# Four edits to the order of work in a two-layer decoder kernel: earlier weight sums, an earlier fifth product, both second-branch gates first, small loads on another queue

## The chip, the cores and the metric

The kernel runs on one core of a Trainium2 chip. The metric is device time in microseconds (us) of one execution, median of several. A core has five engines that run their own instruction streams in order and meet only at semaphores: TensorE (PE, matrix products; PEld is its weight load), VectorE (DVE), ScalarE (ACT), GpSimd (POOL) and SyncE (SP, which here only issues DMAs). An engine's stream is fixed when the kernel is built: an instruction that has to wait holds up all that stand behind it on the same engine.

## The reference, cut to what matters

Two layers; x is 256 positions by 2048 channels, all in float32. Each layer:

```
h = RMSNorm(x);  proj = h @ w_in                  # 2048 x 7680: q | k | v | u, v of the gating unit | gates A | gates B
branch_a = window_attention(q, k, v) @ w_attn_branch        # 1024 x 2048
branch_b = (gelu(u) * spatial(gelu(v))) @ w_sgu_branch      # 1024 x 2048
merged = sigmoid(gates A) * branch_a + sigmoid(gates B) * branch_b
x = x + merged @ w_out                                      # 2048 x 2048
h2 = RMSNorm(x);  x = x + (silu(h2 @ w_gate) * (h2 @ w_up)) @ w_down    # 2048 x 5632, twice; 5632 x 2048
```

## The kernel before, in words

**Three products for one.** Each float32 matrix is split into a high part (rounded to the reduced format fp32r) and a low part (what rounding left), and a product is made of three: high with high, high with low, low with high. That is `three`, lines 345 to 348: the lines PE spends its time in. The weights are split as they arrive: ACT rounds a block of 128 x 1024 (`high`, line 226, tile `whi`), DVE subtracts (`low`, line 234, tile `wlo`). The activations lie in `Unit`s, transposed, with tiles `uh`/`ul` for the parts of the whole and `sh`/`sl` for the parts of sums.

**Jobs, parts and steps.** All weights are cut into jobs (lines 101 to 159), each as a rule 1024 output columns wide, run one after the other by `run` (line 350). A job goes through the input rows in units of 512. One unit of a whole kind is four steps of one weight block ("part") each, with 12 matmuls a step. For jobs with m = 1 the first unit is multiplied in Strassen's manner: seven products of six matmuls each in place of four steps of twelve, in the order of `PRODUCTS` (line 89): 11, t1, t2, 21, t3, 22, t4. Three of the weight blocks are taken as they are (11, 21, 22), four are sums that DVE makes in place (`add`, line 218): t1 = 12 - 11 into an own tile, t2 = 22 - t1 over block 11, t3 = 22 - 12 over block 12, t4 = 21 - t2 over t1's tile. Each layer has 21 such jobs: two of the second branch's gates, two of w_out, and all 17 of the feed-forward part. The others (q, k, v, u, first gates, both branch products) are of the whole kind.

Five PSUM banks serve a Strassen unit (lines 357 to 363): `a`, `q`, `x`, `e`, `y`. ACT copies `a` into `x` after 11, into `e` after t2 and into `y` after t3 (line 380), and `q` into a tile `p5` after 21 (line 383), which DVE adds to `e` and `a` (line 386), before c = 1 of the next unit accumulates into them.

**The stream of weights.** `Stream.fill` (line 238) is called ahead of each step with `upto`, the step's number plus 5. It emits highs for parts up to `upto`, lows for parts below `upto`, and sums for parts below `upto + 2`. There are six `whi` and five `wlo` buffers and four raw weight buffers of 1 MB, so the low of a part can run when PE has finished the part five before it. Lows, sums and all else on DVE share its one queue in the order of emission. `load` (line 174) issues the next weight load on SP when the raw buffer's last part has its low emitted.

**Slots.** What follows from a job's result is written out by hand on a count of slots (`tick`, line 296): a whole step counts 1, a Strassen step 0.5. `soon` runs a function behind the next step's fill, `after(n, f)` n slots later. `evicting` (line 277) places the reads of a job's PSUM banks: both row blocks at the next step for the first 512 columns (c = 0), the second row block later for c = 1, and `then` after it (one, two or three slots). A Strassen job that comes next moves these places (`T1_LATE`, `THEN_LATE`).

**From a branch to w_out.** `branch(gb, j, ...)` (line 1010) multiplies a gate by the branch's product (line 1018, two per c), and its `then_` adds the two branches (`merge`, line 1024) and calls `transposed` (line 479): two DVE transposes (line 432), 16 small DMAs on POOL's queue (line 438) into a tile `tt`, and by slot count a split of what landed: ACT's high (line 535) and DVE's low (line 538). For the first 512 columns (`mT[0]`) w_out's Strassen unit needs sums too: `combine` (line 450), in three slots: `first` with four DVE adds (line 462) and ACT's high (line 464), `second` with DVE's low of the whole (line 457, `ul`) and ACT's high of the sums (line 469), `third` with DVE's low of the sums (line 457, `sl`). It starts 6.7 slots behind `then_`.

The order of jobs is written twice and has to agree: the weights in lines 138 to 159, the runs in lines 970 to 1075. Around the change a layer runs: gates A (two jobs), branch A (two), gate B columns 0 to 1023, branch B of these, gate B columns 1024 to 2047, branch B of these, w_out (two), feed-forward.

**The start.** SP issues eight loads of x between the first four weight loads (lines 306 to 312). POOL issues eight small loads (lines 333 and 630 to 634: two norm rows, the sinks, cosine, sine, three blocks of vector rows), which `tables` (slot 7) and `columns` (slot 12) read. `DMA` issues on SP run in order and each waits for the one eight before it (its semaphore) to land.

Of the kernel before, what the change touches and what calls it, by code (L numbers as in the profile page):

```python
# [14 lines left out]
P = 128  # L15
# [16 lines left out]
CW2 = 2 * CW  # L32
# [18 lines left out]
def hybrid_trunk(ctx: ExitStack, tc: tile.TileContext, x, mix_norm, w_in, q_norm, k_norm, sinks,  # L51
                 sgu_ln_g, sgu_ln_b, w_spatial, b_spatial, w_attn_branch, w_sgu_branch, w_out,
                 ffn_norm, w_gate, w_up, w_down, cosine, sine, out):
    nc = tc.nc
# [32 lines left out]
    O_KV, O_U, O_V, O_GATE = QW, QW + 2 * KVW, QW + 2 * KVW + SW, QW + 2 * KVW + 2 * SW  # L87
    NF = FF // CW
    PRODUCTS = ("11", "t1", "t2", "21", "t3", "22", "t4")

    class Job:

# [10 lines left out]
    def load_of(job, u, h=None):  # L103
        ks = slice(u * CW, (u + 1) * CW) if h is None else slice(u * CW + h * 2 * P, u * CW + (h + 1) * 2 * P)
        loads.append((job, [c[ks, :].rearrange("(k p) n -> p k n", p=P) for c in job.cols]))
        return len(loads) - 1

    def add_job(cols, units=None, m=0):
        job = Job(cols, units, m)
        jobs.append(job)  # L110
        held = {}
        for u in job.units[:m]:
            held[u] = load_of(job, u, 0), load_of(job, u, 1)
        for i, name in enumerate(PRODUCTS if m else ()):
            for n, u in enumerate(job.units[:m]):
                a, b = held[u]
                v = {"11": (a, 0), "12": (a, 1), "21": (b, 0), "22": (b, 1), "new": (f"sum{len(jobs)}_{u}", 0)}
                dst, one, two = {"11": ("11", 0, 0), "22": ("22", 0, 0), "21": ("21", 0, 0),
                                 "t1": ("new", "12", "11"), "t2": ("11", "22", "new"),
                                 "t3": ("12", "22", "12"), "t4": ("new", "21", "11")}[name]  # L120
                parts.append((v[dst], one and (v[one], v[two]), b))
                job.steps.append((name, u, n == m - 1))
        for u in job.units[m:]:
            if not job.pair:
                a = load_of(job, u)
# [12 lines left out]
    for l in range(DEPTH):  # L138
        wl = w_in[l]
        for o in (0, None)[::-1 if l == 0 else 1]:  # L140
            add_job([wl[:, o:o + CW2] if o is not None else wl[:, O_KV:O_KV + CW]])
        for o, m in ((O_V, 0), (O_U, 0), (O_GATE, M_GATE[0]), (O_GATE + CW2, M_GATE[1])):
            add_job([wl[:, o:o + CW2]], m=m)
        for i, o in enumerate((0, CW2)):
            add_job([w_attn_branch[l, :, o:o + CW2]], m=M_ATT[i])
        for i, o in enumerate((0, CW2)):
            add_job([wl[:, O_GATE + D + o:O_GATE + D + o + CW2]], m=M_GATE[2 + i])
            add_job([w_sgu_branch[l, :, o:o + CW2]], m=M_SGU[i])
        for o in (0, CW2):
# [12 lines left out]
    for i, (dst, total, newest) in enumerate(parts):  # L162
        for n in (dst[0], newest, *(w[0] for w in total or ())):
            last_use[n] = i

    class Stream:
# [47 lines left out]
        def add(self):  # L214
            dst, total, _ = parts[self.summed]
            self.summed += 1
            if total:
                nc.vector.tensor_tensor(out=self.raw(dst), in0=self.raw(total[0]), in1=self.raw(total[1]),  # L218
                                        op=ALU.subtract)

        def high(self):
            i = len(self.highs)
            raw = self.raw(parts[i][0])
            hi = whigh.tile([P, 2, CW], F32R, tag="hi", name=nm("whi"))
            for k in self.pieces(i):
                nc.scalar.activation(hi[:, k, :], raw[:, k, :], AF.Copy)  # L226
            self.highs.append(hi)
# [101 lines left out]
    neg_half = const.tile([P, 24], F32, name="neg_half")  # L329
    nc.gpsimd.memset(neg_half, -0.5)  # L330

    def bcast(dst, row):
        nc.gpsimd.dma_start(dst, row.unsqueeze(0).to_broadcast([P, row.shape[0]]))


    def rsqrt(dst, src, n):
# [13 lines left out]
    def run(units, done):  # L350
# [17 lines left out]
        for n, (name, u, at) in enumerate(job.steps):  # L368
# [3 lines left out]
            if name != "whole":  # L372
# [5 lines left out]
                if at:  # L378
                    if name in ("11", "t2", "t3"):
                        nc.scalar.activation({"11": x, "t2": e, "t3": y}[name], a, AF.Copy)  # L380
                    elif name == "21":
                        fifth = temp(name="p5")
                        nc.scalar.activation(fifth, q, AF.Copy)
                    elif name == "t4":
                        for d in (e, a):
                            nc.vector.tensor_tensor(out=d, in0=d, in1=fifth, op=ALU.add)  # L386
                if n < len(job.steps) - 1:
                    tick(0.5)
# [238 lines left out]
        nc.vector.tensor_copy(vcols, pv[:, :NV])  # L627

    def vectors():
        nc.gpsimd.dma_start(cs, cosine.rearrange("(t p) h -> p t h", p=P))  # L630
        nc.gpsimd.dma_start(sn, sine.rearrange("(t p) h -> p t h", p=P))
        nc.gpsimd.dma_start(vrows[:NB, :], mix_norm.rearrange("l (k p) -> (l k) p", p=P))
        nc.gpsimd.dma_start(vrows[NB:2 * NB, :], ffn_norm.rearrange("l (k p) -> (l k) p", p=P))
        nc.gpsimd.dma_start(vrows[2 * NB:, :], b_spatial.rearrange("l g i -> (l g) i"))

    after(3, vectors)
    after(12, columns)

    H2 = HD // 2

    class Layer:
# [7 lines left out]

        def vectors(self):  # L650
            l = self.l
            bcast(self.gn[:, 0, :], q_norm[l])
            bcast(self.gn[:, 1, :], k_norm[l])
            bcast(self.snk, sinks[l])

        def fetch(self, i, eng):

# [312 lines left out]
    for l in range(DEPTH):  # L970
# [142 lines left out]
```

## Time and profile before

| | |
|---|---|
| median of 3 runs | 2488.98 us (2488.92 to 2489.47) |
| the profiled execution | 2486.52 us, span 2484.8 us |
| PE busy | 2464.7 us (99%), 11030 matmuls |
| DVE busy | 1901.5 us (77%) |
| ACT busy | 1359.2 us (55%) |
| POOL busy | 479.5 us (19%) |
| granted TensorE clock | 0.999 |
| read from HBM | 475.27 MB, 192 GB/s over the span |

The span runs from the first to the last instruction; the execution's time is 1.72 us longer, and the median of the runs is another 2.46 us above that. In rows of the timeline the columns are start and duration in us, engine, line, operation, the tile written and the tile read, how many, and in brackets the idle time of the engine before it and what ended it. A matmul's duration there is longer than the distance to the next one, since matmuls overlap; distances of starts tell the pace.

### The profile page before, as it was taken

The page shows a single profiled execution, that of the slowest core. Times are in us where ns is not written, and L with a number is a line of the kernel's source. Part 1 is how long each engine was busy: PE and PEld are TensorE (multiplying, and loading weights), DVE is VectorE, ACT ScalarE, POOL GpSimd, SP SyncE. Part 2 cuts the span into 40 slices and gives each one's busy share as a digit, 9 for nine tenths or more (in the row PEclk, how much of TensorE's full clock was granted, in tenths as well). Part 3 has the DMA queues.
Part 4 walks back from the last instruction along what each step waited for, and adds up shares of the span by engine and source line. Part 5 has one row for each costly group of instructions (what it writes and reads, how often), then busy time and mean ns, then how long its engine had stood idle before and what let it go on. Part 6 is the DMA issues. An engine that isn't in the chain of part 4 may idle for free. (4 is left out here: it accounts for less than half of the span.)

```text
span 2484.8 us, 30610 instructions
## 1 busy us (share of the span) xinstructions
PE 2464.7 (99%) x11030; PEld 2023.1 (81%) x11030; DVE 1901.5 (77%) x2135; ACT 1359.2 (55%) x1660; POOL 479.5 (19%) x911
## 2 busy tenths in 40 slices
PE   9999999999999999999999999999999999999999
PEld 7888887788888888888888888877888888888887
DVE  6796667787877787777878956678878776877686
ACT  5455455576655555455654544555756555645554
POOL 1512202231220022002235122022402200220020
PEclk9999999999999999999999999999999999999999
DMA  8645656666565656566676546565756656565654
GB/s 280 227 157 169 204 196 205 205 200 223 195 233 173 234 187 233 191 219 206 216 231 214 166 160 214 192 201 187 251 189 230 211 197 209 196 221 184 213 192 164
DMA packets 161880, 507.71 MB, mean 204 GB/s; under 512 B 22016, under 2 KB 24672, under 8 KB 161728
## 3 DMA queue, kind: packets, MB, share of 16 engines
q1 hardware_dynamic: 133408, 476.87, 56.7%
q0 software_dynamic: 28000, 28.62, 3.8%
q8 instruction: 86, 1.41, 0.2%
q14 instruction: 66, 0.54, 0.1%
q10 hardware_dynamic: 320, 0.27, 0.0%
HBM read 475.27 MB, written 2.10 MB: 192 GB/s over the span
## 5 line engine op out<-in xcount | busy, mean ns | idle before, releaser
L234 DVE TENSOR_TENSOR wlo<-raw,whi 128x1024 fp32r<-128x1024 f32 (+1 forms) x940 | 1129.5, 1217 | 502.7 <-PE acc L347 415.8
L226 ACT ACTIVATE whi<-raw 128x1024 fp32r<-128x1024 f32 (+1 forms) x940 | 983.3, 1056 | 843.0 <-PE acc L348 773.6
L346 PE MATMUL acc<-whi,uh 128*128 128x512 f32 x3164 | 1243.2, 393 | 7.1 <-DVE acc L386 4.6
L347 PE MATMUL acc<-wlo,uh 128*128 128x512 f32 x3164 | 1232.7, 390 | 3.1 <-DVE wlo L234 3.1
L348 PE MATMUL acc<-whi,ul 128*128 128x512 f32 x3164 | 1232.3, 389 | 0.0
L438 POOL DMA_DIRECT2D tt<-blk x800 | 393.1, 498 | 1721.8 <-DVE blk L432 1042.6
L346 PEld LDWEIGHTS acc<-whi,uh 128*128 128x128 f32 x3164 | 594.2, 188 | 146.2 <-DVE acc L386 13.1
L348 PEld LDWEIGHTS acc<-whi,ul 128*128 128x128 f32 x3164 | 594.4, 188 | 125.0
L347 PEld LDWEIGHTS acc<-wlo,uh 128*128 128x128 f32 x3164 | 594.6, 188 | 124.0 <-DVE wlo L234 3.7
L226 ACT ACTIVATE whi<-sum 128x1024 fp32r<-128x1024 f32 x84 | 89.2, 1062 | 96.6 <-PE acc L348 61.2
L346 PE MATMUL acc<-whi,sh 128*128 128x512 f32 x336 | 132.7, 395 | 5.0 <-ACT acc L380 5.0
L347 PE MATMUL acc<-wlo,sh 128*128 128x512 f32 x336 | 131.0, 390 | 0.0
L348 PE MATMUL acc<-whi,sl 128*128 128x512 f32 x336 | 130.9, 390 | 0.0
L234 DVE TENSOR_TENSOR wlo<-sum,whi 128x1024 fp32r<-128x1024 f32 x84 | 102.5, 1221 | 8.7 <-PE acc L347 8.7
L346 PEld LDWEIGHTS acc<-whi,sh 128*128 128x128 f32 x336 | 63.0, 188 | 23.7 <-ACT acc L380 11.1
L380 ACT ACTIVATE acc<-acc 128x512 f32<-128x512 f32 x126 | 73.7, 585 | 10.0 <-PE acc L348 10.0
L348 PEld LDWEIGHTS acc<-whi,sl 128*128 128x128 f32 x336 | 63.1, 188 | 13.4
L347 PEld LDWEIGHTS acc<-wlo,sh 128*128 128x128 f32 x336 | 63.1, 188 | 12.5
L538 DVE TENSOR_TENSOR ul<-tt,uh 128x1024 fp32r<-128x1024 f32 x38 | 46.4, 1222 | 17.9 <-ACT uh L535 16.1
L535 ACT ACTIVATE uh<-tt 128x1024 fp32r<-128x1024 f32 x38 | 40.3, 1059 | 34.6 <-DMA tt<-blk 32.5
L386 DVE TENSOR_TENSOR acc<-acc,p 128x512 f32<-128x512 f32 x84 | 54.1, 689 | 0.0
L218 DVE TENSOR_TENSOR raw<-raw,sum 128x1024 f32<-128x1024 f32 x42 | 51.4, 1224 | 1.4
(134 smaller groups left out, 1055.0 us busy)
## 6 DMA issues: line engine op xcount, KB each, us to landing
raw<-in_w_in_dram SPq DMA_DIRECT2D x112, 1024.0 KB, 5.1
raw<-in_w_down_dram SPq DMA_DIRECT2D x88, 1024.0 KB, 6.7
raw<-in_w_gate_dram SPq DMA_DIRECT2D x80, 1024.0 KB, 6.0
raw<-in_w_up_dram SPq DMA_DIRECT2D x80, 1024.0 KB, 6.2
raw<-in_w_out_dram SPq DMA_DIRECT2D x32, 1024.0 KB, 6.8
tt<-blk POOLq DMA_DIRECT2D x800, 32.0 KB, 5.1
raw<-in_w_attn_branch_dram SPq DMA_DIRECT2D x16, 1024.0 KB, 6.2
raw<-in_w_sgu_branch_dram SPq DMA_DIRECT2D x16, 1024.0 KB, 5.8
```

Source lines behind the costliest of these rows:

```text
L218: nc.vector.tensor_tensor(out=self.raw(dst), in0=self.raw(total[0]), in1=self.raw(total[1]), op=ALU.subtract)
L226: nc.scalar.activation(hi[:, k, :], raw[:, k, :], AF.Copy)
L234: nc.vector.tensor_tensor(out=lo[:, k, :], in0=raw[:, k, :], in1=hi[:, k, :].bitcast(F32), op=ALU.subtract)
L346: nc.tensor.matmul(ps, a, hi, start=first, stop=False, skip_group_check=True)
L347: nc.tensor.matmul(ps, a, lo, start=False, stop=False, skip_group_check=True)
L348: nc.tensor.matmul(ps, b, hi, start=False, stop=last, skip_group_check=True)
L380: nc.scalar.activation({"11": x, "t2": e, "t3": y}[name], a, AF.Copy)
L386: nc.vector.tensor_tensor(out=d, in0=d, in1=fifth, op=ALU.add)
L438: nc.gpsimd.dma_start(blocks(d)[:, :, i] if whole else d[:, i].rearrange("p k t c -> p (k t) c"), src)
L535: nc.scalar.activation(blocks(unit.hi), tv, AF.Copy)
L538: nc.vector.tensor_tensor(out=blocks(unit.lo), in0=tv, in1=blocks(unit.hi).bitcast(F32), op=ALU.subtract)
```

## The change

It has four parts.

1. Sums: each sum gets a lead of its own (t1 and t2: 1, t3: 3, t4: 4 parts more than `upto`, in place of 1 for all), and a condition: the part whose weight block it overwrites (11 for t2, t1 for t4) must have its low emitted. For t1 and t2 the place stays as it was; t3's sum is emitted two fills earlier, beside t2's, and t4's three fills earlier, right behind t1's low. Parts without a sum pass up to `upto + 4`.
2. Fifth product: DVE adds it to `a` and `e`, in this order, behind the matmuls of 22, and no longer to `e` and `a` behind those of t4.
3. Job order: gate B of columns 0 to 1023, gate B of columns 1024 to 2047, then the two branch B jobs, then w_out. Between the `then_` of the first branch B job and w_out there is now one job of eight whole steps; before, there was a gate job as well.
4. Small loads: the eight of the first layer are issued by SP, at slot 1, behind the first four weight loads; the second layer's three stay on POOL, one slot earlier.

```diff
+    SUM_AHEAD = {"t1": 1, "t2": 1, "t3": 3, "t4": 4}
...
-                parts.append((v[dst], one and (v[one], v[two]), b))
+                over = {"t2": "11", "t4": "t1"}.get(name)
+                at[name, u] = len(parts)
+                parts.append((v[dst], one and (v[one], v[two], at.get((over, u), -1), SUM_AHEAD[name]), b))
...
             add_job([wl[:, O_GATE + D + o:O_GATE + D + o + CW2]], m=M_GATE[2 + i])
+        for i, o in enumerate((0, CW2)):
             add_job([w_sgu_branch[l, :, o:o + CW2]], m=M_SGU[i])
...
+        def due(self, upto):
+            if self.summed == len(parts):
+                return False
+            total = parts[self.summed][1]
+            if not total:
+                return self.summed < upto + 4
+            return self.summed < upto + 1 + total[3] and len(self.parts) > total[2]
...
-                elif self.summed < min(upto + 2, n):
+                elif self.due(upto):
                     self.add()
...
-                    elif name == "t4":
-                        for d in (e, a):
+                    elif name == "22":
+                        for d in (a, e):
                             nc.vector.tensor_tensor(out=d, in0=d, in1=fifth, op=ALU.add)
...
     def vectors():
-        nc.gpsimd.dma_start(cs, cosine.rearrange("(t p) h -> p t h", p=P))
+        nc.sync.dma_start(cs, cosine.rearrange("(t p) h -> p t h", p=P))
...
-    after(3, vectors)
+    after(1, vectors)
...
+            eng = nc.gpsimd if l else nc.sync
+            bcast(eng, self.gn[:, 0, :], q_norm[l])
...
-        after(2, pl.vectors)
+        after(1, pl.vectors)
...
         for j in (0, 2):
             gate(gb, j)
+        for j in (0, 2):
             branch(gb, j, spa.sguT, merge)
```

More of the change, by code (lines that the diff above doesn't have):

```diff
@@ L112, in add_job @@
         for u in job.units[:m]:
-            held[u] = load_of(job, u, 0), load_of(job, u, 1)
+                held[u] = load_of(job, u, 0), load_of(job, u, 1)
+        at = {}
         for i, name in enumerate(PRODUCTS if m else ()):
@@ L162, in hybrid_trunk @@
     for i, (dst, total, newest) in enumerate(parts):
-        for n in (dst[0], newest, *(w[0] for w in total or ())):
+        for n in (dst[0], newest, *(w[0] for w in (total or ())[:2])):
             last_use[n] = i
@@ L330, in hybrid_trunk, with bcast @@
     nc.gpsimd.memset(neg_half, -0.5)
-    def bcast(dst, row):
-        nc.gpsimd.dma_start(dst, row.unsqueeze(0).to_broadcast([P, row.shape[0]]))
+    def bcast(eng, dst, row):
+        eng.dma_start(dst, row.unsqueeze(0).to_broadcast([P, row.shape[0]]))
     def rsqrt(dst, src, n):
@@ L629, in vectors @@
     def vectors():
-        nc.gpsimd.dma_start(cs, cosine.rearrange("(t p) h -> p t h", p=P))
[L631 to L634, printed above, removed]
-    after(3, vectors)
+        nc.sync.dma_start(cs, cosine.rearrange("(t p) h -> p t h", p=P))
+        nc.sync.dma_start(sn, sine.rearrange("(t p) h -> p t h", p=P))
+        nc.sync.dma_start(vrows[:NB, :], mix_norm.rearrange("l (k p) -> (l k) p", p=P))
+        nc.sync.dma_start(vrows[NB:2 * NB, :], ffn_norm.rearrange("l (k p) -> (l k) p", p=P))
+        nc.sync.dma_start(vrows[2 * NB:, :], b_spatial.rearrange("l g i -> (l g) i"))
+    after(1, vectors)
     after(12, columns)
@@ L651, in vectors @@
             l = self.l
-            bcast(self.gn[:, 0, :], q_norm[l])
-            bcast(self.gn[:, 1, :], k_norm[l])
-            bcast(self.snk, sinks[l])
+            eng = nc.gpsimd if l else nc.sync
+            bcast(eng, self.gn[:, 0, :], q_norm[l])
+            bcast(eng, self.gn[:, 1, :], k_norm[l])
+            bcast(eng, self.snk, sinks[l])
         def fetch(self, i, eng):
```

## The prediction

> **What bounds the kernel now.** First the page:
>
> ```profile
> span 2484.8 us, 30610 instructions
> PE 2464.7 (99%) x11030; PEld 2023.1 (81%) x11030; DVE 1901.5 (77%) x2135; ACT 1359.2 (55%) x1660; POOL 479.5 (19%) x911
> ```
>
> PE is the bound, and nothing in the change alters its matmuls; only time in which PE waits can go. Next, who waits for whom, on PE and then on ACT:
>
> ```profile
> PE acc L346 <- ACT acc L380: 5.0, 4, 1.4
> PE acc L346 <- DVE acc L386: 4.6, 4, 1.2
> PE acc L347 <- DVE wlo L234: 3.1, 2, 2.5
> ACT whi L226 <- DVE sum L218: 35.4, 38, 2.4
> ```
>
> Four long waits for a bank copy, four for the fifth product, two in the start; and ACT often waits for a sum. These views miss short waits, since matmuls overlap, so I take the pace from the timeline of PE: the first matmul of step t1 in successive Strassen jobs, from gate B of the first layer on.
>
> ```profile
> 330.22 0.39 PE L346 MATMUL acc<-whi,sh 128*128 128x512 f32 x1
> ...
> 394.16 0.39 PE L346 MATMUL acc<-whi,sh 128*128 128x512 f32 x1
> ...
> 461.23 0.39 PE L346 MATMUL acc<-whi,sh 128*128 128x512 f32 x1
> ...
> 461.68 0.39 PE L348 MATMUL acc<-whi,sl 128*128 128x512 f32 x1
> ...
> 506.53 0.39 PE L346 MATMUL acc<-whi,sh 128*128 128x512 f32 x1
> ...
> 549.19 0.39 PE L346 MATMUL acc<-whi,sh 128*128 128x512 f32 x1
> ...
> 591.89 0.39 PE L346 MATMUL acc<-whi,sh 128*128 128x512 f32 x1
> ...
> 634.09 0.39 PE L346 MATMUL acc<-whi,sh 128*128 128x512 f32 x1
> ...
> 677.01 0.39 PE L346 MATMUL acc<-whi,sh 128*128 128x512 f32 x1
> ```
>
> Matmuls start 0.227 us apart (0.45 over two), so a Strassen step lasts 1.36 us and a whole step 2.72. Gate job plus branch job takes 63.94 us the first time and 67.07 the second: the second gate job loses 3.13. From w_out's first job to its second are 45.30, where 591.89 to 634.09 shows 42.20 for the same work: 3.10 lost. The next two lose 0.46 and 0.50 (42.66, 42.70), and 634.09 to 677.01 loses 0.72 (42.92). The job before it, an "up" job that follows a gate job, loses nothing.
>
> Where the big ones come from, in w_out's first job (PE, ACT, DVE):
>
> ```profile
> 466.64 0.50 PE L346 MATMUL acc<-whi,sh 128*128 128x512 f32 x1 [1.17 <-ACT acc L380]
> 475.12 0.50 PE L346 MATMUL acc<-whi,uh 128*128 128x512 f32 x1 [1.21 <-DVE acc L386]
> ```
>
> ```profile
> 464.10 1.06 ACT L226 ACTIVATE whi<-sum 128x1024 fp32r<-128x1024 f32 x1 [2.09 <-DVE sum L218]
> ```
>
> ```profile
> 449.02 1.23 DVE L234 TENSOR_TENSOR wlo<-raw,whi 128x1024 fp32r<-128x1024 f32 x1 [0.36 <-issue]
> 450.28 1.22 DVE L218 TENSOR_TENSOR raw<-raw,sum 128x1024 f32<-128x1024 f32 x1
> ...
> 454.47 1.23 DVE L234 TENSOR_TENSOR wlo<-raw,whi 128x1024 fp32r<-128x1024 f32 x1 [1.49 <-PE acc L347]
> 455.61 1.22 DVE L218 TENSOR_TENSOR raw<-raw,raw 128x1024 f32<-128x1024 f32 x1
> 456.75 1.28 DVE L1018 SCALAR_TENSOR_TENSOR gate<-gate,acc 128x512 f32<-128x512 f32 x2
> 458.06 1.23 DVE L1024 TENSOR_TENSOR gate<-gate,gate 128x1024 f32<-128x1024 f32 x1
> 459.32 1.31 DVE L432 STREAM_TRANSPOSE blk<-gate 128x512 f32<-128x512 f32 x2
> 460.55 2.32 DVE L234 TENSOR_TENSOR wlo<-raw,whi 128x1024 fp32r<-128x1024 f32 x2
> 462.78 1.22 DVE L218 TENSOR_TENSOR sum<-raw,raw 128x1024 f32<-128x1024 f32 x1
> ...
> 474.37 1.29 DVE L386 TENSOR_TENSOR acc<-acc,p 128x512 f32<-128x512 f32 x2
> ```
>
> DVE is late behind the previous job's results; t4's sum runs at 462.78, ACT waits 2.09 for it, and the copy of `a` into `e` stands behind that on ACT: PE waits. Later the adds of the fifth product (474.37) stand behind merge, transposes and a low.
>
> **Gate B's second job.** It now follows a gate job, whose results only ACT reads; no product, merge or transposes lie on DVE there. That is the up-behind-gate pattern (42.20). Gain 3.13 a layer, **-6.3 us**. If two gate jobs do disturb each other, the nearest row is 42.92: -4.8.
>
> **Sums and fifth product in the other Strassen jobs.** t4's sum leaves the crowded stretch (1.14 us, the distance 454.47 to 455.61) for a whole step with 2.72 us of PE time and 2.4 of DVE work, so ACT's high finds it ready and the copies come on time. The adds now stand ahead of merge or transposes. They wait for ACT's `y` copy and for 22's last matmul; behind them on DVE wait only lows for steps five ahead. By the order of jobs five per layer follow an up job (0.72 each) and about five in all follow as the two after w_out's first do (0.48): 10 x 0.72 + 5 x 0.48 = 9.6. I take **-9.1**; bounds 0 (sums come no earlier in fact) and -9.6.
>
> **w_out's first job.** Here the reorder costs. `mT[0]`'s combine, until now hidden in the second gate job's whole steps, has one branch job of eight steps left. By slots `first` falls behind that job's sixth step, `second` behind the seventh, `third` behind the eighth, the last. Prices:
>
> ```profile
> 412.08 0.42 DVE L462 TENSOR_TENSOR sums<-tt 128x256 f32<-128x256 f32 x1
> ...
> 413.67 1.23 DVE L234 TENSOR_TENSOR wlo<-raw,whi 128x1024 fp32r<-128x1024 f32 x1
> ...
> 417.52 1.22 DVE L457 TENSOR_TENSOR sl<-sums,sh 128x1024 fp32r<-128x1024 f32 x1
> ```
>
> Four adds take 1.59, each low 1.14 to 1.22. On the clock of the quoted rows, with distances from them, DVE would run: low 11 at 449.02, t2's sum 450.28, t3's sum 451.42, t1's low 452.55, t4's sum 453.81, the four adds 454.95, t2's low 456.54, two products 457.68, `ul` 458.99, merge 460.14, transposes 461.40, low 21 462.63, `sl` 463.77, done 464.99. The first matmul that reads `sl` is the third of t1, due at 461.68: PE waits 3.3 us. `ul` is done at 460.2, in time for PE's 460.3. From then on PE is late itself: t3's low, 22, t4 and the adds come out 0.3 us or more ahead of it. With 0.2 for short waits the job loses 3.5 in place of 3.1: **+0.8** for two layers. Bounds: 0.5 lost per job if DVE catches up before t1 (-5.2), 6 if it is 2.5 us later than I count (+5.8).
>
> `first` also needs the gather:
>
> ```profile
> 476.95 1.06 ACT L535 ACTIVATE uh<-tt 128x1024 fp32r<-128x1024 f32 x1 [0.64 <-DMA tt<-blk]
> ```
>
> This one landed 16.3 us after its transposes (459.32 + 1.31). `mT[0]`'s transposes would end near 437.6 (ten whole steps ahead of 459.87, plus a low, two products, merge, transposes), so it lands at 453.9, 1.0 us ahead of the adds. A thin cover: each us of lateness beyond it is a us of PE.
>
> A wait of 3.3 us may also cost clock:
>
> ```profile
> 0.00:8.70 8.70, 5.62 (x26) 4.79 (x26) 2.32 (x7) 3.85 (x8) 6.29 (x18) 1.00 0.74 191
> 8.70:12.10 3.40, 3.08 (x7) 2.49 (x8) 0.96 (x2) 1.62 (x3) 0.00 (x0) 0.50 1.04 366
> 12.10:20.00 7.90, 5.35 (x27) 4.20 (x26) 5.40 (x9) 6.28 (x12) 0.00 (x0) 1.00 1.05 407
> ```
>
> (Stretch, length, PE busy with its count, then the other engines, granted clock, DMA.) The clock fell to 0.50 for 3.4 us after a stretch in which PE was busy 5.62 of 8.70 us, but stayed 1.00 across the start's wait of 2.5 us, with 5.35 of 7.90. A fall costs half of 3.4, 1.7 us. Whether 3.3 us suffice depends on what stands around them; I take one fall in two jobs: **+1.7** (bounds 0 and +3.4). The Trainium skill, "TensorE: Matmul & The Clock Gate", section "HAM oscillation — how this bites in real kernels", has it that the clock halves after PE idles for more than about 3.4 us; by that rule 3.3 us would pass in both, and the sum would be 1.7 lower. The trace does not quite agree: PE idled 3.1 us in all ahead of 8.70, in pieces, and the clock fell.
>
> **Small loads.**
>
> ```profile
> 17.54 17.19 SPq L197 DMA_DIRECT2D raw<-in_w_in_dram  x5
> 28.73 2.01 ACT L226 ACTIVATE whi<-raw 128x1024 fp32r<-128x1024 f32 x2
> raw<-in_w_in_dram SPq DMA_DIRECT2D x112, 1024.0 KB, 5.1
> cs<-in_cosine_dram POOLq DMA_DIRECT2D x1, 32.0 KB, 7.0
> ```
>
> They leave POOL, whose next work is far off, and stand on SP ahead of the fifth weight load (17.54). That one may have to wait until a small one lands: an estimate of 17.54 + 7.0 = 24.5 at the latest, and 5.1 for itself, 29.6. ACT first reads it at 28.73, without a wait; 0.9 us there is covered, since a high stands about five steps ahead of its matmuls. `tables` reads the small ones only at slot 7, seven steps of 2.72 us or more behind the first. So **0**, between +1.0 (cover gone) and -0.5 (the first loads no longer share the DMA engines with the small ones, but PE's 2.5 us in the start are a wait for DVE).
>
> **Sum.** -6.3 - 9.1 + 0.8 + 1.7 + 0 = -12.9 us. The profiled execution (2486.52, span 2484.8) would come to 2473.6; it lies 2.46 below the median, so the median goes from 2488.98 to **2476**.
>
> **Rivals.** *DVE catches up at w_out* (its engine has idle time in the whole steps before; against it, five lows, four sums and the rest of the list above, 18 us of work in 13.6): w_out loses 0.5, no clock falls, -6.3 - 9.1 - 5.2 = -20.6: 2468.4. *w_out loses 6 a job and the clock falls in both*: -6.3 - 9.1 + 5.8 + 3.4 = -6.2: 2482.8; for it speaks the thin cover of 1.0 us. *The sums move in program order only*, DVE reaching them no earlier and the short waits staying: -6.3 + 0.8 + 1.7 = -3.8: 2485.2; against it, the 1.49 us that DVE idles before 454.47. *Slower: the gather of `mT[0]`*. DVE stands at `first`, with all lows behind it, until the gather lands. The rest gains 15.4, or 7.7 a layer, so the job would have to lose 10.8, with `first` 7.3 us late: a gather of 24.6 us in place of 16.3. At 28 us each job loses 14, 2488.98 - 15.4 + 21.8 = 2495.4. Nothing that I saw takes so long.
>
> **How the numbers follow.** Forecast 0.60 (of it no fall of the clock 0.20, 2474.3; one 0.25; two 0.15, 2477.7); catching up 0.13; 6 a job 0.12; order only 0.10; slower 0.05. The range reaches from the second case to just past the third: 2468 to 2483.5. About 0.2% (5 us) can be told from no change: faster is under 2484, which holds the first three, less a little: 0.84; same 0.11; slower 0.05.
>
> **What would show it.** Right: second gate job at 42.2 from the first; 42.2 nearly everywhere in the feed-forward part; ACT's wait for sums nearly gone; PE L386 waits gone; a new PE wait L348 on DVE L457 in w_out's t1, twice, of about 3.3. Wrong: w_out's wait well off 3.3 or in another step; 42.9 remaining; the first steps later than before.

## The result, and the profile after

The whole change runs in 2478.68 us (median of 5 runs, 2475.12 to 2479.46), the kernel before in 2489.39 (5 runs, 2488.92 to 2489.80): 10.7 us less, a ratio of 0.9954 with a 95% interval of 0.9940 to 0.9969. The profiled execution after is the median one, 2478.68 with a span of 2477.0. The profiled execution before was a quick one (2486.52, span 2484.8), so between the two profiles only 7.8 us are to be found, and these are what the rows below account for.

The page of the profile after:

```profile
span 2477.0 us, 30669 instructions
PE 2457.7 (99%) x11030; PEld 2029.2 (82%) x11030; DVE 1903.3 (77%) x2135; ACT 1356.0 (55%) x1660; POOL 473.9 (19%) x903
```

Who waits for whom, on PE (in total, times, longest):

```profile
PE acc L362 <- DVE sl L471: 6.1, 2, 3.1
...
PE acc L360 <- DVE xs L974: 1.8, 1, 1.8
...
PE acc L360 <- ACT acc L394: 1.2, 1, 1.2
```

and on ACT:

```profile
ACT uh L549 <- DMA tt<-blk: 38.0, 18, 5.0
ACT tt L545 <- DMA tt<-blk: 32.9, 12, 4.7
...
ACT whi L240 <- DVE sum L223: 15.6, 9, 1.7
```

(Lines have moved by 14 or so: L360 to L362 are the three products, L400 the fifth product's add, L471 the low in `combine`.) PE no longer waits for the fifth product, and only once for a bank copy. ACT waits for sums 9 times in place of 38. Two waits are new: for `sl`, twice 3.1 us, where the prediction put it; and for a result that stands behind a gathered tile. ACT's waits for gathered tiles were 32.5 and 11.3 us before and are 38.0 and 32.9 now.

The pace, from the timeline of PE, the same first matmuls of t1 as before (first layer):

```profile
330.28 0.39 PE L360 MATMUL acc<-whi,sh 128*128 128x512 f32 x1
...
372.44 0.39 PE L360 MATMUL acc<-whi,sh 128*128 128x512 f32 x1
...
458.56 0.39 PE L360 MATMUL acc<-whi,sh 128*128 128x512 f32 x1
...
505.70 0.39 PE L360 MATMUL acc<-whi,sh 128*128 128x512 f32 x1
...
547.86 0.39 PE L360 MATMUL acc<-whi,sh 128*128 128x512 f32 x1
...
632.55 0.39 PE L360 MATMUL acc<-whi,sh 128*128 128x512 f32 x1
...
674.71 0.39 PE L360 MATMUL acc<-whi,sh 128*128 128x512 f32 x1
```

The second gate job comes 42.16 us behind the first. From w_out's first job to its second are 47.14 (45.30 before), then 42.16, and in the feed-forward part 42.16 from 632.55 to 674.71, where 42.92 stood. Grouped, the distances of these starts account for the whole difference; the last column is the 17 jobs from w_out's second to the last.

| from gate B's first t1 to w_out's second | first layer | second layer | from there to the last t1, both layers |
|---|---|---|---|
| before | 176.31 | 176.29 | 711.76, 711.73 |
| whole change | 175.42 | 175.38 | 707.21, 708.34 |
| sums alone | 172.70 | 172.72 | 706.98, 706.87 |
| fifth product alone | 173.62 | 173.26 | 710.69, 710.40 |
| new order alone | 178.92 | 178.28 | 711.71, 711.69 |
| all but the new order | 170.00 | 174.31 | 707.73, 707.03 |

Before to whole change: -0.9, -0.9, -4.55 and -3.4. From the last t1 of the first layer to the first of the second the whole change takes 346.09 in place of 344.59, 1.5 more, and a new wait stands there (below); ahead of the first t1 and behind the last it takes 0.4 more. The sum is -7.85, the difference of the spans. The gain is in the jobs that the new order does not touch. Around the new order two layers gain 1.8 together, and sums alone gain 7.2 there.

In w_out's first job, on PE and then on DVE:

```profile
458.79 0.40 PE L361 MATMUL acc<-wlo,sh 128*128 128x512 f32 x1
462.24 0.50 PE L362 MATMUL acc<-whi,sl 128*128 128x512 f32 x1 [3.06 <-DVE sl L471]
```

```profile
452.45 0.42 DVE L476 TENSOR_TENSOR sums<-tt 128x256 f32<-128x256 f32 x1 [0.43 <-DMA tt<-blk]
...
456.25 1.22 DVE L471 TENSOR_TENSOR ul<-tt,uh 128x1024 fp32r<-128x1024 f32 x1
457.39 1.22 DVE L1039 TENSOR_TENSOR gate<-gate,gate 128x1024 f32<-128x1024 f32 x1
458.64 1.31 DVE L446 STREAM_TRANSPOSE blk<-gate 128x512 f32<-128x512 f32 x2
459.87 1.18 DVE L248 TENSOR_TENSOR wlo<-raw,whi 128x1024 fp32r<-128x1024 f32 x1
460.97 1.22 DVE L471 TENSOR_TENSOR sl<-sums,sh 128x1024 fp32r<-128x1024 f32 x1
```

DVE runs in the order that the prediction wrote out: `ul`, merge, transposes, a low, `sl`. From merge to the start of `sl` are 3.58 us, foretold as 3.63 (463.77 less 460.14). PE stands for 3.1. Even the thin cover of the gather shows: the adds wait 0.43 for it. What came on top is the clock:

```profile
459.40:462.80 3.40, 0.56 (x2) 0.49 (x3) 3.40 (x4) 1.84 (x2) 2.31 (x5) 1.00 0.10 29
462.80:466.20 3.40, 3.40 (x10) 2.61 (x9) 3.40 (x5) 1.06 (x1) 3.36 (x8) 0.51 0.63 125
```

(Stretch, length, busy time of PE and the other engines with counts, granted clock, DMA share, GB/s.) For 3.4 us behind the wait the granted clock is 0.51, and 10 matmuls lie in a stretch that at 0.227 us from one to the next holds 15. The second layer's job shows the same, from 1691.7 to 1695.0.

And the new wait between the layers, on ACT, DVE and PE:

```profile
1240.65 1.71 ACT L545 ACTIVATE tt<-tt,vcols 128x256 f32<-128x256 f32 x4 [4.72 <-DMA tt<-blk]
...
1243.49 1.23 DVE L552 TENSOR_TENSOR ul<-tt,uh 128x1024 fp32r<-128x1024 f32 x1 [3.65 <-ACT uh L549]
```

```profile
1248.82 0.50 PE L360 MATMUL acc<-whi,uh 128*128 128x512 f32 x1 [1.75 <-DVE xs L974]
```

ACT stands at the split of a gathered unit until the 16 DMAs have landed, DVE at the low of it, and the eviction of the bank that PE needs (`xs`, at 1248.09 on DVE) stands behind that.

### The profile page after: what moved, and what is told of

The parts are those of the page before. It is cut to its first block, busy times and chain, and to the rows that moved or that the text cites. A ratio compares the mean times of both kernels' runs of the same rounds, so it can differ in the third digit from the quotient of the medians.

```text
span 2477.0 us, 30669 instructions
## 1 busy us (share of the span) xinstructions
PE 2457.7 (99%) x11030; PEld 2029.2 (82%) x11030; DVE 1903.3 (77%) x2135; ACT 1356.0 (55%) x1660; POOL 473.9 (19%) x903
## 4 chain that ended last, share of the span: by engine, by line
PE 48%; DMA 1%; DVE 1%; POOL 0%; ACT 0%; issue 0%; DVEq 0%; ACTq 0%; POOLq 0%
PE acc L360 16%; PE acc L362 16%; PE acc L361 16%; DMA tt<-blk 1%; PE po L853 0%; PE psc L811 0%; PE ppt L842 0%; DVE wlo L248 0%; POOL tt L452 0%; PE psg L939 0%; DVE blk L446 0%; ACT tt L545 0%; DVE sums L476 0%; DVE gate L1033 0%; DVE gate L1039 0%
## 5 line engine op out<-in xcount | busy, mean ns | idle before, releaser
L360 PE MATMUL acc<-whi,uh 128*128 128x512 f32 x3164 | 1239.5, 392 | 3.5 <-DVE xs L974 1.8
L362 PE MATMUL acc<-whi,ul 128*128 128x512 f32 x3164 | 1232.7, 390 | 0.1
L360 PEld LDWEIGHTS acc<-whi,uh 128*128 128x128 f32 x3164 | 594.6, 188 | 131.2 <-issue 2.7
L362 PEld LDWEIGHTS acc<-whi,ul 128*128 128x128 f32 x3164 | 594.3, 188 | 125.4 <-DVE ul L471 0.9
L362 PE MATMUL acc<-whi,sl 128*128 128x512 f32 x336 | 132.5, 394 | 6.1 <-DVE sl L471 6.1
L360 PE MATMUL acc<-whi,sh 128*128 128x512 f32 x336 | 132.0, 393 | 1.2 <-ACT acc L394 1.2
L362 PEld LDWEIGHTS acc<-whi,sl 128*128 128x128 f32 x336 | 63.7, 190 | 20.3 <-DVE sl L471 7.0
L360 PEld LDWEIGHTS acc<-whi,sh 128*128 128x128 f32 x336 | 63.6, 189 | 15.3 <-ACT acc L394 2.0
L400 DVE TENSOR_TENSOR acc<-acc,p 128x512 f32<-128x512 f32 x84 | 54.1, 689 | 0.0
L223 DVE TENSOR_TENSOR sum<-raw,raw 128x1024 f32<-128x1024 f32 x42 | 51.5, 1225 | 1.4
```

The lines of the kernel that those rows point to most:

```text
L360: nc.tensor.matmul(ps, a, hi, start=first, stop=False, skip_group_check=True)
L362: nc.tensor.matmul(ps, b, hi, start=False, stop=last, skip_group_check=True)
```

## The experiments

Theory at the outset: sums and fifth product gain in all Strassen jobs; the new order gains in gate B and pays in w_out. The rival: what the new order is credited with comes from the sums already. Differences are of medians, against runs of the kernel before on the same chip; the ratio has its 95% interval.

**The four parts alone.** First the sums, with leads and condition as in the change:

```diff
+    SUM_AHEAD = {"t1": 1, "t2": 1, "t3": 3, "t4": 4}
...
-                elif self.summed < min(upto + 2, n):
+                elif self.due(upto):
                     self.add()
...
```

> The kernel before with the earlier sums alone. My theory: ACT's wait for t4's sum goes, and with it the waits for the bank copies (1.33 us in each of the four jobs that lost 3.1; about 0.3 in each of the ten that lost 0.72); the adds of the fifth product still stand behind merge or transposes on DVE, and their waits stay or grow a little, since PE arrives sooner. So 5 to 8 us faster than before. Rival: the sums are the whole gain of the Strassen jobs, and the place of the adds makes no difference: 13 to 15 us faster.

Measured 2470.85 us (2469.66 to 2474.40), 16.8 less than before; ratio 0.9933 (0.9921 to 0.9946). One part alone gains at least as much as the whole (the intervals just overlap; the spans are 2468.4 and 2477.0). It is more than either side expected: the theory had the waits for the adds stay everywhere, and they don't. Of the waits in the Strassen jobs only the fifth product's is left on PE's list:

```profile
PE acc L359 <- DVE acc L399: 4.2, 4, 1.1
```

These stand in each gate B second job and w_out first job; by the distances of t1 each of the four costs 1.35 us (65.28 and 43.51 in the first layer, where 63.92 and 42.16 show no loss). In the feed-forward part (706.98, 706.87 in the table, 4.8 less than before in each layer) the adds cost nothing any more, though they stand where they stood: with t4's sum made early, DVE reaches them in time. So the sums cure nearly all of what both edits were credited with there.

Then the fifth product:

```diff
-                    elif name == "t4":
-                        for d in (e, a):
+                    elif name == "22":
+                        for d in (a, e):
```

> The kernel before with the fifth product added behind 22 alone. My theory: the waits for the adds go (1.4 to 1.5 us in four jobs, 0.35 in ten, 0.2 in five), those for the bank copies stay: 8 to 10 us faster. Rival: the copies' lateness carries over and the adds, now ahead of a low, delay the lows: no more than 3 us faster.

Measured 2478.87 us, 8.8 less, as the theory had it; ratio 0.9963 (0.9949 to 0.9976). The waits for the add are gone, those for the bank copies are not:

```profile
PE acc L346 <- ACT acc L380: 6.7, 6, 1.4
```

The new order, on the sums and adds of before (first the weights, then the runs):

```diff
             add_job([wl[:, O_GATE + D + o:O_GATE + D + o + CW2]], m=M_GATE[2 + i])
+        for i, o in enumerate((0, CW2)):
             add_job([w_sgu_branch[l, :, o:o + CW2]], m=M_SGU[i])
...
         for j in (0, 2):
             gate(gb, j)
+        for j in (0, 2):
             branch(gb, j, spa.sguT, merge)
```

> The kernel before with both second gates first, and nothing else. My theory: the second gate job gains 3.1 per layer, but w_out's first job has the combine, the late t4 sum and the late adds together and loses 5 to 7 us in place of 3.1, with a fall of the clock in part of them: between 2 us faster and 2 us slower than before, and a wait of PE L348 on DVE L457 of about 2 us per layer. Rival: the combine is hidden as before and the reorder gains its 6.3 us.

Measured 2494.19 us, 6.5 more than before, where between 2 more and 2 less was expected; ratio 1.0024 (1.0014 to 1.0034). By PE's timeline the second gate job comes at 42.2 from the first, as it should, but w_out's first job takes 49.5 in place of 45.3:

```profile
PE acc L349 <- DVE sl L458: 6.1, 2, 3.1
PE acc L347 <- DVE acc L387: 3.2, 2, 2.2
```

It keeps w_out's wait for the fifth product and adds the one for `sl`, which is 3.1 us in each layer where about 2 was expected. Alone, the new order costs.

Last the small loads:

```diff
-        nc.gpsimd.dma_start(cs, cosine.rearrange("(t p) h -> p t h", p=P))
+        nc.sync.dma_start(cs, cosine.rearrange("(t p) h -> p t h", p=P))
...
-    after(3, vectors)
+    after(1, vectors)
```

> The kernel before with the small loads on SP alone. My theory: no difference, within 0.5 us, since PE's waits in the start are on DVE and ACT work that stands behind PE's own first step; the first matmul at 8.0 us and the start's long wait of 2.5 us stay. Rival: the first weights land sooner without the small packets and the start gains 1 to 2 us, or the fifth weight load, now issued 4 us later, costs as much.

Measured 2489.49 us; ratio 1.0006 (0.9997 to 1.0014): no difference in the total. One gather of this kernel lands late all the same, which the next experiment shows.

**All but the new order.** Sums, fifth product and small loads, with the order of before (the weights' order goes back as well):

```diff
...
         for j in (0, 2):
             gate(gb, j)
-        for j in (0, 2):
             branch(gb, j, spa.sguT, merge)
```

> The changed kernel with the order of jobs undone: sums, fifth product and small loads only. My theory now: the sums alone left 1.32 us per job in four jobs, the waits for the adds (5.3 us in all); with the adds behind 22 these go too, so 4 to 6 us faster than the sums alone, 20 to 23 us faster than before: the reorder takes back about 10 us of the change. Rival: the sums alone hold the whole gain, about 17 us faster than before, and the adds give nothing more.

Measured 2470.63 us (2465.49 to 2470.93), 17.8 less; ratio 0.9925 (0.9913 to 0.9938). In the first layer the stretch of gate B and w_out takes 170.00 us, which is 6.3 less than before and 5.4 less than with the new order: no gap of over 0.1 us is left between its matmuls. In the second layer 4.3 of this are lost again. The longest of PE's waits behind gathers, and the gather behind it, from its transposes on DVE to its split on ACT:

```profile
PE acc L359 <- ACT uh L548: 2.1, 1, 2.1
```

```profile
1678.60 1.30 DVE L445 STREAM_TRANSPOSE blk<-gate 128x512 f32<-128x512 f32 x2
...
1701.40 1.06 ACT L548 ACTIVATE uh<-tt 128x1024 fp32r<-128x1024 f32 x1 [7.52 <-DMA tt<-blk]
```

This gather reached its split 21.5 us after its transposes (1678.60 + 1.30), where the same one took 16.4 with the sums alone; each time ACT stood waiting for it. So the gain does not come as 20 us or more, and the rival was nearer: a gather is the next wait.

What makes this one late is the fourth part of the change. With the small loads alone the same gather takes 20.9 us, where it took 16.2 before (1695.02 to 1715.88, and 1693.26 to 1709.49). On POOL its DMAs begin like this, first before and then with the small loads alone:

```profile
1693.80 6.85 POOL L438 DMA_DIRECT2D tt<-blk  x14 [41.12 <-PE acc L347]
```

```profile
1695.56 0.50 POOL L438 DMA_DIRECT2D tt<-blk  x1 [44.74 <-PE acc L347]
1698.92 3.91 POOL L438 DMA_DIRECT2D tt<-blk  x8 [2.87 <-issue]
```

Behind the first DMA of the batch POOL pauses for 2.87 us in which it waits for nothing that the profile shows, and the last of the 16 is issued 15.0 us after the transposes in place of 10.7. All ten profiles with the small loads on SP have this pause at this place in the second layer, and the four others have none there, though single pauses of the same length stand elsewhere. What the pause is stays open. In the whole change the gather takes 18.3 us and PE does not wait for it; here PE does. Sums and fifth product without the small loads were not run. An estimate from the first layer, where this pause is missing (170.00 against 174.31): about 4 us less than this kernel.

**Can the new order be made to pay?** The whole change with `combine` in two slots, `sl` ahead of the merge:

```diff
-        def third():
-            low(flat(unit.shi), flat(unit.slo), flat(s4))
...
-        for i, fn in enumerate((first, second, third)):
+        for i, fn in enumerate((first, second)):
```

> The changed kernel, whole, with the combine in two slots: ACT's high of the sums stands in the first, DVE's low of the sums directly behind that of the whole in the second, ahead of merge and transposes. My theory: the low of the sums ends about 458.6 on the clock of the changed kernel's trace, where PE needs it at 459.0; the wait of 3.2 us and the fall of the clock behind it (1.7 us) both go, 5 us in each of two jobs: 8 to 10 us faster than the changed kernel, 18 to 21 faster than before. Rival: the wait moves to another late piece of work on DVE (the gather's landing, merge, the bank's eviction), and less than 4 us are gained.

Measured 2482.18 us, ratio 0.9973 (0.9965 to 0.9982), no better than the whole change (the profiled execution, 2484.74, is the slowest of the runs). The wait for `sl` is gone, and other work is late in its place, on PE and on ACT:

```profile
PE acc L360 <- ACT acc L394: 5.5, 7, 1.0
...
PE acc L360 <- ACT uh L547: 3.0, 1, 3.0
PE acc L360 <- DVE xs L972: 2.5, 1, 2.5
```

```profile
463.10 0.58 ACT L394 ACTIVATE acc<-acc 128x512 f32<-128x512 f32 x1 [1.70 <-DVE gate L1031]
```

In each layer's w_out a bank copy needs a bank that DVE has yet to evict from the branch job, and the branch's product is now behind `sl`. The two longest waits are of another kind: the 3.0 us stand behind a gather in the second layer's w_out, for which ACT waits 9.0, and the 2.5 us between the layers at the place of the whole change's 1.8; a clock of 0.50 follows both, for 6.8 and 3.4 us. So the rival was right: in this one placement of `sl` other late work takes over.

**Gathers.** The whole change with the split of a gathered unit one slot later, and with its low one slot later too:

```diff
-            after(n, split)
-            after(n + 1, lower)
+            after(n + 1, split)
+            after(n + 1 + 1, lower)
```

> The changed kernel with the split of every gathered unit without sums one slot later on ACT and DVE. My theory: in the changed kernel ACT stands at a split whose gather hasn't landed (4.7 us near 1236, 4 us near 1757), since PE now goes through the slots faster while the gather takes as long; the two PE waits that follow (1.9 and 1.4 us) go: 2 to 4 us faster than the changed kernel. Rival: the waits are not due to the gather, or the later split delays what reads it: no difference or slower.

Measured 2479.30 us, ratio 0.9968 (0.9955 to 0.9980): level with the whole change, and the 2 to 4 us did not come. The waits behind gathers are gone from PE's list, and the lows of the units (`ul`) are late in their place, 2.0 us in eight waits.

Then the last two edits in one kernel, `combine` in two slots and the split and low one slot later:

> Both edits of the two runs before in the changed kernel. My theory: they add, 11 to 14 us faster than the changed kernel, 21 to 24 faster than before. Rival: with PE earlier still, the gathers are late by as much again, and no more than the two-slot combine's gain is left.

Measured 2479.17 us (2476.49 to 2487.76), ratio 0.9964 (0.9950 to 0.9977). Also level, and more spread out; the profiled execution is the slowest of its runs, so nothing is read from it.

Without the new order, the split one slot later and the low left where it is:

```diff
-            after(n, split)
+            after(n + 1, split)
             after(n + 1, lower)
```

> The change without its new job order, and ACT's split of a gathered unit one slot later, in the slot of DVE's low of the same unit, which stays where it is. Theory (the landing of gathers is what is left: ACT stands in order at a split, with highs and bank copies behind it): of the 5.0 us that PE loses there without the new order, some 4 come back: 2466 to 2467, 21 to 22 us faster than before, with ACT's waits for gathered tiles under 20 us in all where they were 51.0 and 28.8. Rival (those waits cost nothing that PE does not lose anyway): 2470 to 2471, as without the new order, or slower, because DVE now waits for ACT at each low.

Measured 2469.65 us (2468.94 to 2472.17), 17.7 less than before; ratio 0.9929 (0.9916 to 0.9943). The theory expected 4 us more than without the edit, and they did not come. ACT's waits for gathers are down from 79.8 to 19.9 us as foretold, yet PE waits at the same place for the same gather, 1.5 us in place of 2.1:

```profile
1700.91 0.50 PE L359 MATMUL acc<-whi,uh 128*128 128x512 f32 x1 [1.53 <-ACT uh L548]
```

What PE needs there is the gathered unit itself; the landing is late, 20.5 us after the transposes. Elsewhere the standing has only changed engines. DVE's low now comes right behind the split and waits for it (4.08 us ahead of 1754.92), and ACT's waits for sums go from 15.6 to 35.1 us. What the second layer's w_out got back (172.62 for the stretch in place of 174.31) the jobs behind it lost (708.74 in place of 707.03). The rival was right.

The opposite, the split and its low one slot earlier:

```diff
-            after(n, split)
-            after(n + 1, lower)
+            after(n - 1, split)
+            after(n, lower)
```

> The same kernel with the split and its low one slot earlier than they stand, so that the suspected wait is lengthened: ACT stands up to 2.7 us longer for each of the gathers that land late. Theory (landing of gathers): PE loses several us more than without the new order, 2474 to 2480. Rival (ACT's standing is covered by the highs made ahead): unchanged, 2470 to 2471.

Measured 2478.39 us, ratio 0.9962 (0.9949 to 0.9974), 8.9 less than before where the kernel without this edit is 17.8 less: the loss came as foretold. ACT's wait at the split nearly doubles (51.0 in 19 waits without the edit):

```profile
ACT uh L548 <- DMA tt<-blk: 95.9, 20, 10.7
```

So an engine that stands at a gather does cost, if it stands long enough; as the slots were written, most of it was covered. Of the 7.6 us between the two profiles, 1.9 are from the start (below).

**The clock.** The whole change, with 13 more matmuls into a spare bank where PE waits for `sl` (a repeat of a product, which nobody reads):

```diff
...
+                        for r in range(13):
+                            nc.tensor.matmul(fill, ah, hi[:, k, :], start=True, stop=True, skip_group_check=True)
+                        nc.tensor.matmul(p, al, hi[:, k, :], start=False, stop=False, skip_group_check=True)
...
```

> The whole change, with 13 more matmuls of 512 columns (a repeat of t1's first product into a spare bank that nobody reads) between the second and the third matmul of t1 in the first job of w_out of each layer, so that PE works through the 3.1 us in which it waits for DVE's low of the sums. If PE's idle time is what halves the clock there, the clock stays at 1.00 in both jobs and the time falls by about 2 x 1.7 = 3.4 us against the whole change, to some 2475. If the clock falls for another reason, the pitch of 0.427 us stays and the time is that of the whole change, 2478 to 2479.

On PE in w_out's first job, and the stretches of time there:

```profile
460.75 0.39 PE L395 MATMUL acc<-wlo,sh 128*128 128x512 f32 x1
460.98 3.13 PE L397 MATMUL fill<-whi,sh 128*128 128x512 f32 x13
464.20 0.50 PE L398 MATMUL acc<-whi,sl 128*128 128x512 f32 x1
```

```profile
459.40:462.80 3.40, 3.31 (x14) 2.74 (x15) 3.37 (x5) 2.72 (x4) 0.77 (x2) 1.00 0.11 29
462.80:466.20 3.40, 3.30 (x15) 2.40 (x14) 3.40 (x5) 1.13 (x2) 3.38 (x8) 1.00 0.23 63
```

`sl` comes no sooner (464.20 is 3.45 behind 460.75, against 462.24 and 458.79), but the clock stays at 1.00, with 15 matmuls in the second stretch in place of 10. In the second layer's job it does not fall either. PE's idle time is shown to be what halves the clock. In the first layer the job takes 46.04 us in place of 47.14, 1.1 of the 1.7 that were expected. The median is 2479.21 us, ratio 0.9966 (0.9954 to 0.9979), and so the 3.4 us that I expected did not come in the total: in the second layer the distance is 47.14 as before, with two waits of 0.6 and 0.7 us in the whole steps of w_out's first job that the whole change did not have, and this profile's start was 1.8 us slower.

**The new order, priced once more**, with the later split of two experiments ago and the change's order:

```diff
-            after(n, split)
+            after(n + 1, split)
             after(n + 1, lower)
```

> The whole change, its new job order included, with the split of gathered units one slot later and DVE's low in its old place. Against the kernel with the same split and the old job order this prices the new order alone. Theory (the new order costs: 5 us in the first job of w_out of each layer, of which a halved clock 1.7): 2475 to 2477, some 10 us above the one with the old order. Rival (the new order costs only by the gathers that it hurries): within 3 us of it, 2466 to 2470.

Measured 2480.54 us, ratio 0.9970 (0.9959 to 0.9982), against 2469.65 and 0.9929 (0.9916 to 0.9943) for the same kernel with the old order, on the same chip: 10.9 us for the order alone, and the intervals are apart. The difference is the 10 us expected; the time itself lies above the 2475 to 2477. The waits for `sl` are back, 6.0 us in two, and the clock falls behind both.

## Why the prediction was right, and where it was wrong

The forecast was 2476.0 in a range of 2468 to 2483.5; 2478.68 lies in it, and the change is faster by more than the noise. By its steps:

- *Gate B's second job, -6.3.* It came 42.16 behind the first as foretold. But the step credited the gain to the new order, and that failed: without the new order the sums and the fifth product take the same 3.1 us away (63.92 from gate job to gate job and from there to w_out, in place of 63.94 and 67.07).
- *The other Strassen jobs, -9.1.* Near. They gained 4.55 and 3.4, the second after 1.3 us given to a new wait for a bank copy (1.16 in PE's list, at 1779.20); ACT had stood 4.0 us for a gather 18 us earlier and was still late, but that this is the cause is not shown. The mechanism was right too, but the fifth product is hardly needed for it: sums alone take 4.8 and 4.9 there.
- *w_out's first job, +0.8.* The wait for `sl` is in the foretold matmul, twice, at 3.1 us where 3.3 was forecast. As a difference from before the sum is sound; as the price of the new order it is not. The step set 3.5 against the 3.1 lost before, as though those were lost in any case. Sums and fifth product remove them by themselves (42.16 in place of 45.30 in the first layer without the new order). The price of the wait is the whole 3.1 in each job, 6.2.
- *The clock, +1.7.* The size was off: it fell in both jobs, 3.4, with PE idle for 3.1 us. The Trainium skill, "TensorE: Matmul & The Clock Gate", section "HAM oscillation — how this bites in real kernels", puts the limit at gaps of more than about 3.4 us, and by it the clock would have stayed. Here the measurement differs and decides: a gap of 3.06 us with 0.56 us of work in the 3.4 around it was enough. What decides is not the length alone (last section): of the two waits in the start that the prediction compared, one left PE 1.44 us of work in a window of 3.41 us and the clock fell, the other was cut in two and it stayed.
- *Small loads, 0.* Right for the total: 1.0006 (0.9997 to 1.0014). That they delay a gather of the second layer (20.9 us in place of 16.2) was not foreseen; it costs PE once the jobs ahead of it are faster.
- *Not foreseen:* the landing of other gathers. The prediction looked at `mT[0]`'s alone. The stretch between the layers, with the late one before 1240.65, takes 1.5 more.

Gate B, w_out and clock were forecast at -3.8 together and came to -1.8; the rest at -9.1 and came to -7.9; the stretch between the layers took 1.5 back, start and end 0.4. That is -12.9 against -7.8 between the profiles; the medians differ by 10.7, since the profiled execution of before was 2.9 below its median and that of after was not below its own. So it is in part luck that the median came within 2.7 us of the forecast: between the profiles the sum was 5.1 off.

The error that the total hides is in the attribution. Sums alone, -16.8; fifth product alone, -8.8; both with the small loads, -17.8; the new order, +6.5 alone and 7.1 (whole change) or 10.9 (with the later split, on one chip) on top of the others. The first two remove much the same waits, so their gains do not add; and in the second layer the gather that the small loads delay hides what the fifth product still gains in the first (172.70 to 170.00). The new order sheds a wait that they shed anyway, and puts 3.1 us of waiting and 1.7 of halved clock into each layer's w_out. Dropping it gives the best kernels of this study, 2469 to 2471 us; the three of them (sums alone, all but the order, that with the later split) can't be told apart.

What stays open: what POOL's pause of 2.87 us is, and what sums and fifth product give without the small loads. The pause goes with the small loads, not with the fifth product or the order: with the fifth product alone, and the old order, this gather takes 16.2 us and there is no pause. The run that would price it, sums and fifth product with the small loads left on POOL, wasn't made.

## What to carry to other kernels

Price each edit of a bundle on top of the others: a wait that one edit removes is no longer there to be traded by the next, and a reorder that looked like a small gain was the one part that cost by itself. A part that shows no difference alone can still cost beside the others, as the small loads' late gather did. Where a chain of hand-written slots is shortened, look at what is counted in slots but takes a fixed time (here a gather of 16 to 22 us): it is the next wait, and to let another engine stand in front of it, or stand there later, brought nothing here. And a wait on a PE that is otherwise full can cost more than its length: here 1.7 us of halved clock for 3.1 of idling.

## What the runs showed of the hardware

The length of a wait does not decide alone whether the clock falls. In the whole change with the split and its low one slot later, PE waits 2.9 us for `sl` in w_out of each layer, and the clock falls in the first layer only. Here are two stretches of 3.41 us of each layer, with PE's wait in them:

```profile
460.21:463.62 3.41, 1.39 (x6) 1.15 (x7) 3.41 (x4) 0.29 (x2) 3.13 (x7) 1.00 0.17 48
463.62:467.03 3.41, 3.41 (x10) 2.67 (x9) 3.41 (x5) 2.21 (x3) 3.41 (x8) 0.50 0.73 182
```

```profile
1685.59:1689.01 3.42, 1.86 (x9) 1.20 (x7) 3.39 (x4) 2.60 (x3) 0.41 (x1) 1.00 0.03 10
1689.01:1692.42 3.41, 2.06 (x9) 1.73 (x10) 3.41 (x5) 0.79 (x1) 0.54 (x2) 1.00 0.03 10
```

The edges are not chosen freely. Within each of the fourteen profiles all changes of the granted clock lie whole multiples of 3.413 us apart, so they mark out windows of that length, and from execution to execution these windows lie elsewhere against the program. In the first layer most of the wait lies in one window, PE is busy for 1.39 us of it, and the next window runs at 0.50. In the second layer an edge cuts the wait in two, PE is busy for 1.86 and 2.06, and the clock stays. All fourteen profiles agree. Leave out the first and the last 12 us and take the windows at full clock: in 18 of them PE is busy for 1.61 us or less, and the window behind each is at 0.50; in all others it is busy for 1.63 us or more, and no fall follows. So a shorter wait than 2.9 us can do it too. In the kernel without the new order it was 2.14 us at the late gather, in one piece:

```profile
1699.28:1702.69 3.41, 1.27 (x6) 0.75 (x5) 0.20 (x1) 1.29 (x2) 1.66 (x4) 1.00 0.92 321
1702.69:1706.10 3.41, 3.24 (x8) 2.03 (x9) 3.29 (x3) 2.61 (x3) 3.17 (x7) 0.50 0.54 108
```

The long wait of PE in the start, between 13.5 and 18.8 us, with 3.03 us from one matmul to the next in every profile, halved the clock in some executions and not in others. First the kernel with nothing but the small loads changed, then the whole change, which issues them alike:

```profile
13.53:16.94 3.41, 1.34 (x10) 0.95 (x8) 1.83 (x5) 2.70 (x6) 0.00 (x0) 1.00 1.05 407
16.94:20.36 3.42, 2.94 (x7) 2.36 (x8) 3.42 (x5) 3.42 (x7) 0.00 (x0) 0.50 0.93 327
```

```profile
12.29:15.70 3.41, 2.18 (x14) 1.65 (x12) 0.99 (x3) 1.86 (x5) 0.00 (x0) 1.00 1.05 387
15.70:19.11 3.41, 2.09 (x9) 1.75 (x10) 3.41 (x6) 3.41 (x7) 0.00 (x0) 1.00 1.05 399
```

In the one the wait lies in a single window, in the other an edge cuts it. Five of the fourteen profiles have this second fall (the new order alone, the small loads alone, both late edits together, the split earlier, the filled wait), and their first t1 comes at 332.0 to 333.3 us, against 329.8 to 330.8 in the nine others. So some 2 us of what single profiles differ by come from the start, whatever was changed.
